# A planned order for the state-space mixer, and where the rows of the modulation are summed

## The chip, the cores and the metric

The kernel runs on one core of a Trainium2 chip. The metric is the time of one execution on the device, in microseconds (us). Three runs of the kernel before the change are shown, and one more execution was taken with the profiler. Engine names are those of the profile: PE is TensorE (PEld its weight loads), DVE is VectorE, ACT is ScalarE, POOL is GpSimd, SP is SyncE, which only issues transfers here.

## The reference

Two layers over a sequence of 1024 rows with 1024 channels, batch 1, all in float32. Each layer has a token mixer and a squared-ReLU MLP, both behind an RMS norm that is modulated by a vector c.

```
cs = silu(c)
for i in range(2):
    mod = cs @ w_ada[i] + b_ada[i]                      # 6 rows of 1024
    sh1, sc1, gt1, sh2, sc2, gt2 = split(mod, 6)
    h = rmsnorm(x, norm_mix[i]) * (1 + sc1) + sh1
    y = s5_mixer(h, ...) if i == 0 else gla_mixer(h, ...)
    x = x + gt1 * y
    h = rmsnorm(x, norm_mlp[i]) * (1 + sc2) + sh2
    x = x + gt2 * (relu(h @ w_ff1[i]) ** 2 @ w_ff2[i])
return rmsnorm(x, norm_final)
```

The mixer of layer 0 (S5) is a diagonal complex state-space layer: 64 groups of 16 channels, each with 64 complex states. It ends with a gated product: z = gelu(y), (val, gate) = split(z @ w_glu, 2), val * sigmoid(gate), where w_glu is 1024 x 2048.

## The kernel before, in words

The work runs through four large stages on one core: the mixer of layer 0 (up to some 170 us of the span), its gated product (to some 390 us), the two MLPs with the mixer of layer 1 between them. Matrix products of full precision are made of three products of split operands (a high and a low half, `split`, L106: ScalarE copies the high half, VectorE subtracts it for the low one).

**The mixer's steps.** The mixer is cut into eight blocks of eight groups each. The work on a block is written as generators whose steps run one at a time, and a string, `S5ORD` (L739), says in which order: each word is a letter and a block, and each time that it comes up the next step of that generator is traced. Inside the brackets the instructions of VectorE, ScalarE, GpSimd and TensorE stand in exactly this order in each engine's queue; an engine that meets a step whose input isn't there waits, with all that is queued behind it. The letters, with the engines of their steps in order:

- `g` (`group`, L511; b is a quarter, 0 to 3): 1 TensorE, 64 matmuls of c with four tiles of w_ada; 2 ScalarE copies; 3 TensorE transposes; 4 VectorE, three small operations; 5 TensorE, a small matmul; 6 ScalarE copies the scale and shift of the groups of two blocks, `gs`.
- `u` (`feed`, L544): 1 ScalarE, eight copies of x by rms into a `wk` buffer; 2 TensorE, eight transposes; 3 ScalarE, eight scalings by `gs` into U.
- `e` (`tab_e`, L573): 1 and 2 VectorE, two products each; 3 and 4 VectorE, a difference each, into E.
- `l` (`tab_lb`, L591): 1 and 2 VectorE, two products each into a `stg` buffer; 3 TensorE, 32 transposes and sums into two `tp` banks of PSUM; 4 ScalarE, two copies into LBT.
- `k` (`tab_k`, L619): 1 TensorE, 32 small products into two `tp` banks; 2 ScalarE, two copies into Ks; 3 VectorE, one small sum; 4 ScalarE issues the write of Ks to `kd` in memory; 5 ScalarE issues the read of `kd` as Tb.
- `p` (`rotation`, L486): 1 VectorE, a sum of phases; 2 VectorE, two operations that take off whole turns; 3 ScalarE, sine, absolute value and sine into the tile rot.
- `s` (`states`, L647): 1 ScalarE, R; 2 TensorE, 32 products of LBT and U; 3 VectorE, four products with rot; 4 VectorE, two sums; 5 VectorE, two scans; 6 VectorE, four products with rot into X.
- `o` (`output`, L691): 1 TensorE, 16 products with Tb; 2 TensorE, 64 products with X and E; 3 ScalarE, two Gelus into z.
- `S`, `T`, `H`, `I`: squares of x, the rms, the phases and the input matrices, once each.

The tag `tp` has two banks of PSUM and `mm` six. The tag `pz` has nine buffers: the last nine of the sixteen tiles of w_ada that the groups read (the last one of group 1, four of group 2, four of group 3) have them first, and then the tiles rot and z take them in turn as they come free. The tag `stg` has three buffers of 128 x 1056 (a load into one moves 512 KB).

**The gated product** (L905 to L939) runs over four quarters j of the columns and eight tiles t of 128 rows. A tile is 24 matmuls of 128 x 512 (`tok_mm`), a sigmoid on ScalarE and products on VectorE. The weights of a quarter come through `stg` (`glu_weights`, eight loads into four tiles in turn), and are split by ScalarE (wh) and VectorE (wl). Before j = 0, and during it, `ztrans` transposes z on TensorE, two groups of four for each tile, and splits it into hT.

**The rows of the modulation.** Two of the 6 rows of layer 0 are made by `group`. Ten rows remain for the list `ADA` (L904); the first six are made in the gated product: (0,2), (1,0), (0,3), (0,4), (0,5), (1,1), each a pair of layer and row. `ada_sum` (L173) loads eight tiles of 128 x 1024 of w_ada through `stg` and adds them up, weighted by silu(c), on VectorE into the tile adacc (one buffer, tag nrow). `ada_row` (L183) sums adacc over the partitions with four matmuls on TensorE (L191), adds the bias on VectorE into a `wk` buffer and, for (0,4) and (1,1), loads a row of norm weights into the same single buffer nrow and multiplies by it; then it writes the row to memory, mod. gt1 (row (0,2)) is read from there after j = 0, the scale and shift of the MLP (rows (0,4) and (0,3)) after j = 2.

Outside the brackets of S5ORD a planner orders the instructions when the kernel is built: at each point an engine takes, of the instructions that its own estimate holds to be ready, the one that was traced first. So the place of a call in the loop is a rank rather than a position. The queues are fixed after that.

Of the kernel before, what the change touches and what calls it, by code (L numbers as in the profile page):

```python
# [43 lines left out]
def trunk_kernel(ctx, tc, x, c, w_ada, b_ada, norm_mix, norm_mlp, s5_a_re, s5_a_im, s5_log_dt, s5_b_re, s5_b_im,  # L44
# [10 lines left out]
    def tt(out, a, b, op, e=None):  # L55
        (e or V).tensor_tensor(out=out, in0=a, in1=b, op=op)  # L56
# [8 lines left out]
    def act(out, a, f, **kw):  # L65
        S.activation(out=out, in_=a, func=f, **kw)  # L66
# [4 lines left out]
    def bank(tag="mm"):  # L71
        return ps.tile([P, 512], F32, tag=tag, name=tag, bufs={"mm": 6, "tp": 2}[tag])
# [40 lines left out]
    def row(src, tag="row", bufs=3, pool="ww"):  # L113
        t = pools[pool].tile([P, 1024], F32, tag=tag, name="row", bufs=bufs)
        nc.sync.dma_start(out=t, in_=src.to_broadcast([P, 1024]))
        return t
# [3 lines left out]
    def openp(name, side):  # L120
        pools[name] = tc.alloc_tile_pool(name=name, bufs=1, side=side, reuse_waits="tile")
        return pools[name]
# [50 lines left out]
    def ada_sum(l, j):  # L173
        acc = pools["ww"].tile([P, 1024], F32, tag="nrow", name="adacc", bufs=1)
        for kt in range(KT):
            w = stage(w_ada[l, kt * P:(kt + 1) * P, 1024 * j:1024 * (j + 1)])
            if kt == 0:
                ts(acc, w, csil[:, 0:1], ALU.mult)
            else:
                stt(acc, w, csil[:, kt:kt + 1], acc, ALU.mult, ALU.add)  # L180
        return acc

    def ada_row(l, j, acc):  # L183

        bt = wk()[:64, :512]
        for q in range(2):
            nc.sync.dma_start(out=bt[32 * q:32 * q + 32, :],
                              in_=b_ada[l:l + 1, 1024 * j + 512 * q:1024 * j + 512 * q + 512].to_broadcast([32, 512]))
        pst = bank()
        for q in range(2):  # L190
            T.matmul(pst[32 * q:32 * q + 32, :], ones, acc[:, 512 * q:512 * (q + 1)], start=True, stop=True)  # L191
        tt(bt, pst[:64, :], bt, ALU.add)
        if (l, j) in scales:
            n = pools["ww"].tile([P, 1024], F32, tag="nrow", name="nrow", bufs=1)[:64, :512]
            for q in range(2):
                nc.sync.dma_start(out=n[32 * q:32 * q + 32, :],
                                  in_=scales[l, j][:, 512 * q:512 * q + 512].to_broadcast([32, 512]))
            stt(bt, bt, 1.0, n, ALU.add, ALU.mult)
        for q in range(2):
            nc.sync.dma_start(out=modr[l][j][:, 512 * q:512 * q + 512], in_=bt[32 * q:32 * q + 1, :])  # L200
# [111 lines left out]
    def small(shape, dt=F32):  # L312
        n_s[0] += 1
        return sp.tile(shape, dt, name=f"s{n_s[0]}")
# [47 lines left out]
    s1 = small(sh1)  # L362
# [23 lines left out]
    s2 = small(sh1)  # L386
# [343 lines left out]
    def glu_weights(j, k2s=range(4)):  # L730
        wg = []
        for k2 in k2s:
            src = s5_w_glu[0, 2 * k2 * P:(2 * k2 + 2) * P, :].rearrange("(k p) (v n) -> p k v n", p=P, v=2)
            h, l = wsplit(None, [(lambda a, k=k: a.rearrange("p (k v n) -> p k v n", k=2, v=2)[:, k],
                                  src[:, k, :, 256 * j:256 * j + 256]) for k in range(2)])
            wg += [(h[:, 512 * k:512 * k + 512], l[:, 512 * k:512 * k + 512]) for k in range(2)]
        return wg

    S5ORD = "[ s0 s1 S7 S6 I0 S2 S3 e0 I0 S5 H1:v S0 S4 S1 e0 T0 H0:v T0 g0 l0 u0:am p0:v e0 e1 g0 g0 e0 u0 g0 u1:am e1 g0 l0 g1 g0 e1 u0 p0 k0 e1 e2 k0 p1:v g1 l0 p0 k0 e2 p1 e2 k0 p1 g2 l1 e2 l0 l1 g2 g1 e3 g2 s0 g1 g2 g1 g3 s0 g1 k0 g2 u1 g2 g3 e3 k1 u2:am e3 s0 k1 u1 l1 k1 s0 k1 p2:v s2 o0 s0 l1 g3 s1 g3 l2 g3 o0 s1 g3 k1 l2 k2 o0 e3 u2 p2 s1 k2 p2 l2 k2 s1 e4 k2 u2 o1 s1 l2 l3 o1 u3:am e4 l3 k2 s3 p3:v k3 e4 o1 s2 p3 e4 u3 e5 k3 p3 l3 s2 u3 k3 s2 l4 k3 l3 s2 u4:am k4 s3 e5 k4 s2 o2 s4 u4 l4 k3 o2 u5:am s3 u4 e5 l4 p4:v k4 e5 o2 p4 s3 k4 l4 e6 p4 k5 s3 s4 l5 o3 k5 s5 s3 u5 k4 u6:am e6 o3 l5 u5 s4 l5 o3 e6 p5:v k5 e6 k5 p5 l5 s4 p5 k6 e7 s5 s4 u6 k6 u7:am o4 l6 s4 k5 s6 u6 e7 o4 l6 s5 l6 o4 e7 p6:v k6 p6 k6 l6 e7 s5 p6 k7 s6 l7 s5 u7 k7 u7 o5 l7 s5 l7 k6 s7 s6 o5 l7 p7:v k7 p7 k7 s6 p7 s7 s6 o5 s7 o6 k7 s6 s7 o6 s7 s7 o6 o7 o7 o7 ]"  # L739

    kinds = {"u": feed, "l": tab_lb, "e": tab_e, "k": tab_k, "p": rotation, "s": states, "o": output, "g": group, "I": inputs}
    gen = {}
# [1 line left out]
    last = {}  # L744
    for n, w in enumerate(S5ORD.split()):
        if w[1:] != "7":
            continue
        last[w[0]] = n
    for n, w in enumerate(S5ORD.split()):
        if w == "[":  # L750
# [34 lines left out]
    def ztrans(t):  # L785
        for q in range(2):
            pt = bank("tp")
            for k in range(4):
                T.transpose(pt[:, P * k:P * k + P], zt[4 * q + k][:, t, :], ident)
            put(zT, t)(q, pt.rearrange("p (k t) -> p k t", k=4))  # L790
# [9 lines left out]
    def tok_mm(pst, hT_, t, w, cs=slice(None)):  # L800
        hh, hl = (hT_[i][:, t] for i in range(2))
        for kt in range(KT):
            mm3(pst, hh[:, kt, :], hl[:, kt, :], w[kt][0][:, cs], w[kt][1][:, cs], kt == 0, kt == KT - 1)
# [61 lines left out]
    def first_half(side):  # L865

        br = openp("br", side)
        return [[br.tile([P, 4, 512], F32R, name=f"{n}{q + 1}1") for n in "hl"] for q in range(2)]

    def second_half(side):  # L870
        return openp("rw", side).tile([P, 2, 4, 512], F32, name="raw")

    def put_block(R, t, xv, g, sh, e=V):

        tk = slice(P * (t % 4), P * (t % 4) + P)

        def evac(q, src):
            if t < 4:
                split(R[q][0][:, :, tk], R[q][1][:, :, tk], src)
            elif q:  # L880
                act(R[2][:, 1, :, tk], src, AF.Copy)
            else:
                tt(R[2][:, 0, :, tk], src, R[2][:, 1, :, tk], ALU.subtract)
        return norm_T(stg()[:, :1024], xv, g, sh, evac, (0, 1) if t < 4 else (1, 0), e)
# [13 lines left out]
    def gated(t, js, u):  # L898

        tt(u, u, gt1[:, js], ALU.mult)  # L900
        xv = xb[:, 7 - t, js]
        tt(xv, xv, u, ALU.add)

    ADA = [(0, 2), (1, 0), (0, 3), (0, 4), (0, 5), (1, 1), (1, 2), (1, 3), (1, 4), (1, 5)]  # L904
    for j in range(4):  # L905
        if j > 0:
            wg = glu_weights(j)
        js = slice(256 * j, 256 * j + 256)
        for t in range(NT):
            pst = bank()  # L910
            tok_mm(pst, zT, t, wg)
            if j == 0:
                if t + 2 < NT:
                    ztrans(t + 2)
                sg = held[t // 4][:, 256 * (t % 4):256 * (t % 4) + 256]
            else:
                sg = pools["ww"].tile([P, 256], F32, tag="sg", name="sg", bufs=3)
            if j < 3 and t in (1, 5):
                acc = ada_sum(*ADA[0])
            if j < 3 and t in ((4, 7) if j == 2 else (3, 7)):  # L920
                ada_row(*ADA.pop(0), acc)
            act(sg, pst[:, 256:], AF.Sigmoid)
            tt(sg, pst[:, 0:256], sg, ALU.mult)
            if j > 0:
                gated(t, js, sg)
            if j == 3:
                xv = xb[:, 7 - t, :]
                put_block(R, t, xv, g2, sh2)
        if j == 0:
            zp.release()  # L930
            openp("mp", "right")
            gt1 = row(modr[0][2])
            for t in range(NT):
                gated(t, js, held[t // 4][:, 256 * (t % 4):256 * (t % 4) + 256])
        if j == 2:
            g2 = row(modr[0][4])
            sh2 = row(modr[0][3])
            pools["mp"].release()
            R = first_half("right") + [second_half("right")]  # L939
# [450 lines left out]
    for w in ORD.split():  # L1390
        t, j = int(w[1]), int(w[2:] or 0)
# [60 lines left out]
    g2 = row(modr[1][4])  # L1452
# [83 lines left out]
```

## Time and profile before

| what | value |
|---|---|
| median of 3 runs | 2189.99 us (2188.33 to 2190.81) |
| the profiled execution | 2189.98 us |
| its span, first to last instruction | 2188.3 us |
| PE busy | 2112.1 us (97%) |
| DVE busy | 1447.4 us (66%) |
| ACT busy | 692.9 us (32%) |
| POOL busy | 397.0 us (18%) |
| mean granted clock of TensorE | 0.987 |

The busy shares are means over stages with different bounds. The profile names lines of the kernel; many operations go through helpers (L56 a product, sum or difference of two tiles on VectorE, L59 a product with a scalar and a second operation, L63 one with a scalar, L66 an operation of ScalarE, L215 to L217 the three matmuls of a full product), so the tiles' names tell them apart. A row of the instructions in order of time gives start, length, engine, line, operation, output<-input, and in square brackets the idle time of the engine before it and what ended it. A row of the chain of waits gives start, length, engine or DMA, and tile and line.

### The profile page before, as it was taken

How to read it: one execution, taken by the hardware profiler on the slowest of the kernel's cores; microseconds unless marked ns; L12 is line 12 of the kernel's file. 1: busy time of each engine (PE TensorE's matmuls, PEld its weight loads, DVE VectorE, ACT ScalarE, POOL GpSimd, SP SyncE). 2: the span in 40 equal slices, each digit the busy share in tenths (PEclk: the TensorE clock that was granted, in tenths of full speed). 3: DMA queues.
4: the chain of work that ended last, by engine and by line, in shares of the span. 5: the costliest groups of instructions: out<-in, count | busy, mean ns of one | idle time of the engine just before them, and what ended most of it. 6: DMA issues, size and time to landing. Idle time of an engine off the chain costs nothing.

```text
span 2188.3 us, 26758 instructions
## 1 busy us (share of the span) xinstructions
PE 2112.1 (97%) x10857; PEld 1726.8 (79%) x10857; DVE 1447.4 (66%) x2004; ACT 692.9 (32%) x1163; POOL 397.0 (18%) x294
## 2 busy tenths in 40 slices
PE   5988999999999999999899999999999999999998
PEld 4887777788888888888687877787788888888886
DVE  8996767966656656656732366738875665665666
ACT  5772114322222222222511443314322222222223
POOL 0000001222213213222500000001122222222223
PEclk9999999999999999999899999999999999999999
DMA  8234670111111111112343114421111111111112
GB/s 257 57 89 166 228 241 23 39 58 58 49 49 58 49 49 58 49 49 75 132 144 100 49 34 143 150 77 38 41 48 49 58 48 49 58 49 49 58 49 106
DMA packets 107655, 176.58 MB, mean 81 GB/s; under 512 B 10462, under 2 KB 76102, under 8 KB 107468
## 3 DMA queue, kind: packets, MB, share of 16 engines
q1 hardware_dynamic: 97164, 168.71, 24.3%
q10 hardware_dynamic: 10368, 6.16, 1.3%
q8 instruction: 85, 1.39, 0.3%
q14 instruction: 38, 0.31, 0.0%
HBM read 164.45 MB, written 10.40 MB: 80 GB/s over the span
## 4 chain that ended last, share of the span: by engine, by line
PE 88%; DVE 6%; DMA 3%; ACT 2%; issue 1%; POOL 0%; SPq 0%; ACTq 0%; POOLq 0%; DVEq 0%
PE mm L216 27%; PE mm L215 27%; PE mm L217 27%; DMA stg<-in_w_ada_dram 1%; DVE tmp L56 1%; PE tp L609 1%; PE mm L1362 1%; PE tp L210 1%; PE mm L1342 1%; PE mm L704 1%; DMA stg<-in_s_w_glu_dram 0%; PE mm L658 0%; DVE adacc L59 0%; DMA stg<-in_gla_w_out_dram 0%; DVE nk L59 0%
## 5 line engine op out<-in xcount | busy, mean ns | idle before, releaser
L56 DVE TENSOR_TENSOR big<-mm,big 128x512 f32<-128x512 f32 x528 | 343.0, 684 | 91.3 <-PE mm L217 86.3
L216 PE MATMUL mm<-w,a 128*128 128x512 f32 x1024 | 386.7, 392 | 0.5 <-DVE w L56 0.5
L217 PE MATMUL mm<-w,a 128*128 128x512 f32 x1024 | 384.8, 390 | 0.0
L215 PE MATMUL mm<-w,a 128*128 128x512 f32 x1024 | 365.1, 390 | 2.6 <-ACT w L66 2.6
L216 PE MATMUL mm<-l,rg 128*128 128x512 f32 x904 | 356.3, 394 | 4.7 <-DVE l L56 4.7
L217 PE MATMUL mm<-h,rg 128*128 128x512 f32 x904 | 355.0, 393 | 0.5 <-DVE rg L56 0.5
L215 PE MATMUL mm<-h,rg 128*128 128x512 f32 x904 | 351.1, 394 | 2.4 <-ACT h L66 1.8
L56 DVE TENSOR_TENSOR wk<-mm,wk 128x512 f32<-128x512 f32 (+1 forms) x100 | 68.8, 688 | 381.5 <-PE mm L217 312.5
L215 PE MATMUL mm<-wh,hT 128*128 128x512 f32 (+1 forms) x768 | 291.1, 381 | 2.5 <-ACT hT L66 1.7
L56 POOL TENSOR_TENSOR wk<-wk 128x512 f32<-128x512 f32 (+1 forms) x122 | 160.3, 1324 | 732.3 <-DVE wl L56 307.4
L217 PE MATMUL mm<-wh,hT 128*128 128x512 f32 (+1 forms) x768 | 290.3, 378 | 0.0
L216 PE MATMUL mm<-wl,hT 128*128 128x512 f32 (+1 forms) x768 | 289.6, 378 | 0.1
L56 POOL TENSOR_TENSOR wk<-wk,row 128x1024 f32<-128x1024 f32 x64 | 163.1, 2549 | 610.2 <-DMA wk<-in_w_ff_dram 405.4
L216 PEld LDWEIGHTS mm<-w,a 128*128 128x128 f32 x1024 | 192.3, 188 | 46.4 <-DVE w L56 7.3
L215 PEld LDWEIGHTS mm<-w,a 128*128 128x128 f32 x1024 | 191.3, 188 | 44.6 <-ACT w L66 3.5
L217 PEld LDWEIGHTS mm<-w,a 128*128 128x128 f32 x1024 | 192.3, 188 | 39.1
L66 ACT ACTIVATE wk<-mm 128x512 f32<-128x512 f32 x140 | 83.4, 597 | 422.7 <-PE mm L217 419.0
L216 PEld LDWEIGHTS mm<-l,rg 128*128 128x128 f32 x904 | 170.6, 189 | 43.1 <-DVE l L56 5.6
L215 PEld LDWEIGHTS mm<-h,rg 128*128 128x128 f32 x904 | 170.2, 188 | 41.5 <-ACT h L66 2.3
L217 PEld LDWEIGHTS mm<-h,rg 128*128 128x128 f32 x904 | 170.5, 189 | 39.0 <-DVE rg L56 0.8
L66 ACT ACTIVATE rg<-wk 128x1024 fp32r<-128x1024 f32 (+1 forms) x126 | 114.2, 952 | 266.1 <-POOL wk L56 264.7
L215 PEld LDWEIGHTS mm<-wh,hT 128*128 128x128 f32 x768 | 144.7, 189 | 40.1 <-issue 3.9
(244 smaller groups left out, 2615.8 us busy)
## 6 DMA issues: line engine op xcount, KB each, us to landing
wk<-in_w_ff_dram SPq DMA_DIRECT2D x128, 512.0 KB
stg<-in_w_ada_dram SPq DMA_DIRECT2D x80, 512.0 KB
stg<-in_gla_w_in_dram SPq DMA_DIRECT2D x17, 512.0 KB
stg<-in_s_w_glu_dram SPq DMA_DIRECT2D x32, 256.0 KB
row<-mod SPq DMA_DIRECT2D x10, 512.0 KB
wada<-in_w_ada_dram SPq DMA_DIRECT2D x9, 512.0 KB
big<-in_x_dram SPq DMA_DIRECT2D x8, 512.0 KB
Tb<-kd ACTq DMA_DIRECT2D x8, 512.0 KB
```

Source lines behind the costliest of these rows:

```text
L56: (e or V).tensor_tensor(out=out, in0=a, in1=b, op=op)
L66: S.activation(out=out, in_=a, func=f, **kw)
L210: ins = T.transpose(pt[:, P * k:P * k + P], h[:, P * (4 * q + k):P * (4 * q + k + 1)], ident)
L215: T.matmul(pst, ah, bh, start=first, stop=False, **kw)
L216: T.matmul(pst, ah, bl, start=False, stop=False, **kw)
L217: return T.matmul(pst, al, bh, start=False, stop=last, **kw)
L609: T.matmul(pts[i][:, P * q:P * q + P], t[i][k][:, P * q:P * q + P], (nident if i < k else ident), start=q == 0 and k == 0, stop=q == 3 and ...
L704: T.matmul(Yp[r][:, P * q:P * q + P], X[rr, i, q, :], E[rr, i // 2, q, :], start=False, stop=(q == 3 and i == 3))
L1342: T.matmul(kvp[c2][hp2][:, 256 * (h % 2):256 * (h % 2) + 256], kz[t % 2][cr, P * h:P * h + P], vo[cr, t, 256 * h:256 * h + 256], start=Tru ...
L1362: T.matmul(op[h // 2][64 * c2:64 * c2 + 64, 256 * (h % 2):256 * (h % 2) + 256], qT[:, h, n0:n0 + 64], Sc[c2][:, h, :], start=True, stop=True)
```

## The change

Two things. The string S5ORD is replaced by another order of the same words (262 of them between the brackets' ends, each as often as before). And the calls of `ada_sum` and `ada_row` stand at other tiles of the gated product: the sums were at tiles 1 and 5 of j = 0, 1 and 2, the rows at tiles 3 and 7 (4 and 7 in j = 2). Now j = 0 has one sum (tile 4) and one row (7), j = 1 two sums (0, 4) and two rows (2, 7), and j = 2 three sums (0, 2, 5) and three rows (1, 4, 7). The order of the rows in ADA stays.

```diff
@@ -736,7 +736,7 @@
             wg += [(h[:, 512 * k:512 * k + 512], l[:, 512 * k:512 * k + 512]) for k in range(2)]
         return wg
 
-    S5ORD = "[ s0 s1 S7 S6 I0 S2 S3 e0 I0 S5 H1:v S0 S4 S1 e0 T0 H0:v T0 g0 l0 u0:am p0:v e0 e1 g0 g0 e0 u0 g0 u1:am e1 g0 l0 g1 g0 e1 u0 p0 k0 e1 e2 k0 p1:v g1 l0 p0 k0 e2 p1 e2 k0 p1 g2 l1 e2 l0 l1 g2 g1 e3 g2 s0 g1 g2 g1 g3 s0 g1 k0 g2 u1 g2 g3 e3 k1 u2:am e3 s0 k1 u1 l1 k1 s0 k1 p2:v s2 o0 s0 l1 g3 s1 g3 l2 g3 o0 s1 g3 k1 l2 k2 o0 e3 u2 p2 s1 k2 p2 l2 k2 s1 e4 k2 u2 o1 s1 l2 l3 o1 u3:am e4 l3 k2 s3 p3:v k3 e4 o1 s2 p3 e4 u3 e5 k3 p3 l3 s2 u3 k3 s2 l4 k3 l3 s2 u4:am k4 s3 e5 k4 s2 o2 s4 u4 l4 k3 o2 u5:am s3 u4 e5 l4 p4:v k4 e5 o2 p4 s3 k4 l4 e6 p4 k5 s3 s4 l5 o3 k5 s5 s3 u5 k4 u6:am e6 o3 l5 u5 s4 l5 o3 e6 p5:v k5 e6 k5 p5 l5 s4 p5 k6 e7 s5 s4 u6 k6 u7:am o4 l6 s4 k5 s6 u6 e7 o4 l6 s5 l6 o4 e7 p6:v k6 p6 k6 l6 e7 s5 p6 k7 s6 l7 s5 u7 k7 u7 o5 l7 s5 l7 k6 s7 s6 o5 l7 p7:v k7 p7 k7 s6 p7 s7 s6 o5 s7 o6 k7 s6 s7 o6 s7 s7 o6 o7 o7 o7 ]"
+    S5ORD = "[ s0 s1 S7 S6 I0 S2 S3 e0 I0 S5 H1:v S0 S4 S1 e0 T0 H0:v T0 g0 l0 u0:am p0:v e0 p0 g0 g0 e0 u0 p0 g0 l0 g0 e1 g1 g0 u1:am p1:v e1 k0 p1 k0 g1 l0 u0 k0 e1 e2 e1 e2 k0 p1 g2 l1 l0 e2 l1 g2 g1 g2 s0 g1 g2 e2 g1 g2 s0 u1 g1 k0 g2 k1 u2:am g3 p2:v s0 k1 g3 l1 u1 k1 s0 p2 k1 s2 o0 l1 s0 p2 g3 s1 g3 l2 g3 o0 g3 s1 k1 l2 k2 o0 s1 u2 e3 k2 u2 s1 l2 k2 e3 k2 u3:am o1 p3:v e3 p3 l2 e3 p3 s1 k3 s2 l3 k2 k3 o1 s3 s2 l3 u3 o1 k3 s2 l3 e4 k3 u3 s2 l3 e4 o2 u4:am p4:v e4 s3 p4 k3 e4 p4 u4 s2 k4 l4 k4 o2 s4 s3 u4 l4 o2 k4 s3 l4 e5 k4 u5:am s3 l4 e5 o3 s5 p5:v e5 s4 p5 k4 e5 u5 p5 s3 k5 l5 k5 o3 u5 s4 u6:am l5 k5 s4 l5 o3 e6 s4 k5 l5 e6 o4 s6 p6:v e6 s5 p6 e6 u6 p6 s4 k6 l6 k5 o4 k6 u6 s5 u7:am l6 k6 s5 l6 o4 e7 s5 k6 l6 e7 o5 s7 p7:v e7 s6 p7 e7 u7 p7 s5 k7 l7 k6 o5 k7 u7 s6 l7 o5 k7 s6 l7 k7 s6 o6 l7 s6 s7 o6 s7 k7 s7 o6 s7 s7 o7 o7 o7 ]"
 
     kinds = {"u": feed, "l": tab_lb, "e": tab_e, "k": tab_k, "p": rotation, "s": states, "o": output, "g": group, "I": inputs}
     gen = {}
@@ -915,9 +915,9 @@
                 sg = held[t // 4][:, 256 * (t % 4):256 * (t % 4) + 256]
             else:
                 sg = pools["ww"].tile([P, 256], F32, tag="sg", name="sg", bufs=3)
-            if j < 3 and t in (1, 5):
+            if (j, t) in ((0, 4), (1, 0), (1, 4), (2, 0), (2, 2), (2, 5)):
                 acc = ada_sum(*ADA[0])
-            if j < 3 and t in ((4, 7) if j == 2 else (3, 7)):
+            if (j, t) in ((0, 7), (1, 2), (1, 7), (2, 1), (2, 4), (2, 7)):
                 ada_row(*ADA.pop(0), acc)
             act(sg, pst[:, 256:], AF.Sigmoid)
             tt(sg, pst[:, 0:256], sg, ALU.mult)
```

## The prediction

> **What bounds the kernel now.** I read the page first, then stretches of 20 us, then the chain of waits, and last each engine's instructions in order of time around the two places that the diff touches.
>
> ```profile
> span 2188.3 us, 26758 instructions
> ...
> PE 2112.1 (97%) x10857; PEld 1726.8 (79%) x10857; DVE 1447.4 (66%) x2004; ACT 692.9 (32%) x1163; POOL 397.0 (18%) x294
> ```
>
> TensorE is busy for 97% of the span, so time can only come from, or go into, the few places where it waits. Here is the part that the diff touches (columns: stretch, length, busy time of each engine, granted clock, DMA share, GB/s):
>
> ```profile
> 20.00:40.00 20.00, 11.45 (x171) 8.78 (x171) 19.55 (x41) 14.13 (x39) 1.97 (x1) 1.00 1.09 349
> ...
> 120.00:140.00 20.00, 18.71 (x269) 17.04 (x269) 19.93 (x32) 17.36 (x38) 0.00 (x0) 1.00 0.32 80
> 140.00:160.00 20.00, 14.30 (x169) 13.43 (x169) 15.72 (x26) 10.86 (x18) 0.00 (x0) 0.88 0.56 124
> ...
> 200.00:220.00 20.00, 20.00 (x97) 15.66 (x96) 12.63 (x17) 4.35 (x9) 0.00 (x0) 1.00 0.44 154
> ```
>
> Up to some 150 us (the mixer's steps) VectorE is the bound: 19.93 of 20 us. From 180 us on (the gated product) it is TensorE: 20.00 of 20, with VectorE at two thirds. So in the mixer a wait of VectorE costs its length; in the gated product only a wait of TensorE does.
>
> **The change, part by part. First the mixer's order.** Both orders hold the same 262 words, so VectorE's work is the same, and only its waits differ. The old order's large waits:
>
> ```profile
> 51.40 2.48 DVE L56 TENSOR_TENSOR tmp<-mm,rot 128x512 f32<-128x512 f32 x4 [1.35 <-PE mm L658]
> ...
> 155.23 2.48 DVE L56 TENSOR_TENSOR tmp<-mm,rot 128x512 f32<-128x512 f32 x4 [4.25 <-ACT rot L66]
> ```
>
> The second goes: p7 now stands before k7, so rotation 7 is ready some 13 us of VectorE work before s7 uses it: -4.25. In its place s7 meets another. After l7's second step VectorE has k7 (0.1), s6's sums (1.2), scans (2.25) and four products (2.4), 6.0 us in all; TensorE has l7 (3.78, row below), o6's 16 products (1.8) and s7's 32 (1.9), 7.5 us: a new wait of +1.5. The last read of kd also comes about 0.5 us too late for o7, an estimate from its write of 6.31 us: +0.5.
>
> ```profile
> 130.35 3.78 PE tp L609 x32
> ...
> 147.12 6.31 DMA kd<-Ks
> ```
>
> The first wait gets worse, and this is the point of the order that I trust most. The chain of waits over the start:
>
> ```profile
> 33.09 1.21 DVE tmp L56 x2
> ...
> 36.09 3.43 PE mm L518 x64
> 39.52 0.61 PE tp L628 x31
> ...
> 40.15 0.29 ACT Ks L66
> ...
> 40.48 3.84 PE tp L609 x32
> 44.32 1.02 PE mm L518 x30
> ...
> 45.37 1.16 ACT rot L66 x2
> ...
> 46.55 0.72 ACT rot L66
> 47.27 0.97 ACT LBT L66 x2
> ...
> 48.79 2.93 PE mm L658 x32
> ```
>
> ```profile
> 31.64 2.43 ACT L66 ACTIVATE wk<-big,s 128x128 f32<-128x128 f32 x8
> ...
> 45.37 1.15 ACT L66 ACTIVATE rot<-tmp 128x512 f32<-128x512 f32 x2 [2.81 <-PE mm L518]
> ```
>
> Rotation 1 waited 2.81 us, until half of group 2's matmuls (1.02 us) was through. The code says why: the rotations and the nine last weights of the groups share the nine buffers pz. Rotation 0 gets the buffer of group 1's last weight, rotation 1 that of group 2's first. In the old order p0's third step stands behind group 1's matmuls; in the new one it stands ahead of them. ScalarE runs its queue in order, so it sits at rotation 0 until 39.52. Behind it are queued rotation 0 (1.88), the copy of group 0 (0.2), u1's eight copies (2.43, in the old order long done) and the first copy of Ks (0.29): Ks is there at 44.32 instead of 40.44. VectorE, which has products of 0.60 each and comes to k0's third step at about 40.5 (8.7 us of steps from 31.8), waits 3.9 us there, and l0's transposes start 3.88 us later, since they need the two PSUM banks that Ks leaves. From there the old chain runs on: 51.72 + 3.88 = 55.6 for the end of s0's products. TensorE has by then sat idle for 4 us, and such a wait slows what follows:
>
> ```profile
> 90.64 1.56 PE L628 MATMUL tp<-E,BB 64*32 64x128 f32 x32 [2.82 <-ACT LBT L66]
> ```
>
> (1.56 us for what took 0.61 above.) I allow -1.0 to +3.2 for the clock, since the old 2.93 of s0 was at the lower clock already, and take 56.5 (54.6 to 58.8). That is 5.1 after the old 51.40, and VectorE has done 1.2 us less by then (g3's and e3's steps come later): the early shift is +6.3 (4.4 to 8.6). Sum of the order: 6.3 - 4.25 + 1.5 + 0.5 = **+4** (2 to 6). If rotation 0 did not wait: -1.35 - 4.25 + 2.0 = -3.6.
>
> **Second, the sums.** The old places of the six rows' matmuls, and of the two sums in the third quarter of the gated product (j = 2):
>
> ```profile
> 229.52 1.05 PE L191 MATMUL mm<-adacc,ones 128*32 128x512 f32 x4
> ...
> 255.20 1.05 PE L191 MATMUL mm<-adacc,ones 128*32 128x512 f32 x4
> ...
> 278.56 1.05 PE L191 MATMUL mm<-adacc,ones 128*32 128x512 f32 x4
> ...
> 307.43 1.05 PE L191 MATMUL mm<-adacc,ones 128*32 128x512 f32 x4
> ...
> 326.88 1.19 PE L215 MATMUL mm<-wh,hT 128*128 128x512 f32 x4 [0.62 <-ACT wh L66]
> ```
>
> ```profile
> 286.73 0.68 DVE L59 SCALAR_TENSOR_TENSOR wk<-wk,nrow 64x512 f32<-64x512 f32 x1 [3.42 <-DMA nrow<-in_norm_mlp_dram]
> 287.45 0.75 DVE L63 TENSOR_SCALAR adacc<-stg,csil 128x1024 f32<-128x1024 f32 x1
> ...
> 302.96 1.28 DVE L59 SCALAR_TENSOR_TENSOR adacc<-stg,csil,adacc 128x1024 f32<-128x1024 f32 x1
> ...
> 309.47 0.73 DVE L63 TENSOR_SCALAR adacc<-stg,csil 128x1024 f32<-128x1024 f32 x1
> ...
> 322.80 1.28 DVE L59 SCALAR_TENSOR_TENSOR adacc<-stg,csil,adacc 128x1024 f32<-128x1024 f32 x1 [0.76 <-DMA stg<-in_w_ada_dram]
> ```
>
> Read as: a row's matmuls run at their place in the code, since TensorE always has work ahead of them. The accumulator adacc has one buffer, so a sum starts only after the row before it (307.43 + 1.05, next sum at 309.47). A sum takes 302.96 + 1.28 - 287.45 = 16.8 us or 322.80 + 1.28 - 309.47 = 14.6; VectorE needs only eight steps of 1.28, the rest is waiting for stg, three buffers of 512 KB. I take S = 15.7. And the weights of the last quarter share stg behind the last sum: it ends at 324.08, and j = 3 starts 2.8 us later with a wait for these weights. That chain is the second bound of this stage, with little slack already.
>
> The diff puts one row into j = 0, two into j = 1, three into j = 2. The fourth row, which needs the nrow buffer too, goes from (1,7) to (2,1), and so two sums and that row stand where one sum stood, between (1,7) and (2,4). New chain: the third row's matmuls at (1,7) end at 279.61, less one row that is no longer ahead (1.05), less 1.5 gained at the start of j = 1 (its first four tiles took 255.20 - 230.57 = 24.6 us, the last four 278.56 - 256.25 = 22.3; the weights come earlier when one sum fewer stands before them): 277.06. Then 1.0 to the fourth sum, S, the fourth row (1.05, and 279.61 to 287.45 = 7.84 to the next sum), S, the fifth row (2.04), S, and 2.8 to the weights (a row's write to mod waits on SP's queue ahead of the next sum's loads; that is in the measured gaps): 291.8 + 3S = 338.9. The old j = 3 starts at 326.88: **+12.0** (8.7 at 14.6, 15.3 at 16.8). TensorE has no other work to put there: the eight tiles end near 325.
>
> At nothing I cost: gt1, which now comes after (0,7), not (0,3); the first tiles of j = 1 fill six PSUM banks before TensorE waits, and without that cover it would cost a row's way, some 8 us. And the first sum's move from tile 1 to tile 4:
>
> ```profile
> 174.24 0.75 DVE L63 TENSOR_SCALAR adacc<-stg,csil 128x1024 f32<-128x1024 f32 x1 [4.90 <-DMA stg<-in_w_ada_dram]
> ...
> 178.59 1.09 PE L789 MATMUL tp<-ident,z 128*128 128x128 f32 x4 [4.12 <-DVE hT L56]
> ```
>
> The sum waits for its load in VectorE's queue with the first tile's hT behind it, and TensorE waits 4.12 for that. But the planner already pulled it ahead of everything up to tile 1, and a place at tile 4 does not forbid that; if it did, up to -4.1.
>
> The profiled execution took 2189.98 us, which is the median of the runs shown (2189.99). Sum: 2189.98 + 4 + 12 = **2206 us**.
>
> **Rivals.** (1) The sums fit. The DMA moved 349 GB/s in 20 to 40 us; eight times 512 KB at that rate are 12.0 us, the chain ends at 327.8, and the loss there is 0.9: 2195. Against it: three buffers never gave a sum under 14 us. The Trainium skill, "DMA: Bandwidth & Descriptors", Specifications, puts the limit of one core's HBM traffic at about 358 GB/s; an estimate by that figure is 11.7 us for a sum and 2194 us for the kernel. The 349 GB/s of the first row agrees with it, but there the loads don't wait for three buffers. (2) Rotation 0 does not wait and the chain stands: 2189.98 - 3.6 + 12 = 2198. Against it: the 2.81. (3) Faster: the new order pays in full. Place: VectorE at 51 and 155 us, -5.6, with s7's wait hidden under an earlier l7. It decides from the point where 291.8 + 3S - 326.88 is below 1.2, that is S under 12.1: 2185 at most. For it: VectorE's waits are the mixer's only loss. (4) The change does nothing in the gated product, because the planner keeps the sums where they were: then only the order counts, 2194. Against it: rows stood at their places in the code each time.
>
> **How the numbers follow.** The forecast 0.58, its own range 2200 to 2213; rival 1 0.10; rival 2 0.15; rival 3 0.10; rival 4 0.07. Range for 8 in 10: 2190 to 2214, which leaves out rival 3 and a chain in which TensorE also stands at a row's matmuls. 0.2% is 4.4 us, about what a measurement of this kernel can tell from no change. Below 2185.6: rival 3 and a tail, 0.12. Within 4.4: rival 4 and half of rival 1, 0.13. Above: 0.75.
>
> **What would show it.** Right: ScalarE's first rot waits some 4 us for L518, VectorE's first product on rot starts at 56 to 57 instead of 51.4, no 4 us wait for rot near the end; six rows' matmuls with the fourth and fifth some 26 us apart or more; j = 3's first products over 10 us late, after a wait for wh. Wrong: sums of 12 us or fewer, or a first rot that starts near 36.

## The result, and the profile after

The changed kernel took 2212.11 us (median of 4 runs, 2209.53 to 2212.9) against 2189.26 (4 runs) of the kernel before beside it: a ratio of 1.0102, interval 1.0084 to 1.0119. It is slower by 22.9 us. Its profiled execution took 2209.53 us, the shortest of the four, so the trace can explain 19.5 us (span 2207.8 against 2188.3) and not the other 3. The head of the page after:

```profile
span 2207.8 us, 26759 instructions
...
PE 2119.2 (96%) x10857; PEld 1729.1 (78%) x10857; DVE 1451.2 (66%) x2004; ACT 692.7 (31%) x1163; POOL 396.4 (18%) x294
```

Stretches of 20 us of the changed kernel (columns as before, the granted clock in the third place from the end):

```profile
40.00:60.00 20.00, 14.68 (x241) 12.94 (x234) 12.73 (x27) 12.46 (x38) 0.00 (x0) 0.83 0.33 101
...
240.00:260.00 20.00, 15.60 (x61) 11.53 (x60) 16.92 (x32) 0.77 (x2) 0.00 (x0) 0.91 0.62 200
...
300.00:320.00 20.00, 19.37 (x74) 14.46 (x75) 10.87 (x16) 0.77 (x2) 0.00 (x0) 0.87 0.73 257
320.00:340.00 20.00, 16.25 (x64) 12.13 (x64) 14.82 (x17) 1.15 (x3) 0.00 (x0) 0.91 0.74 251
```

The first stretch is the early wait of the mixer. The other three are in the gated product, where TensorE had been busy for 20.00, 20.00 and 19.31 of 20 us at clock 1.00: it now misses 4.40 us in the first of them, 0.63 in the second and 3.75 in the third, and its mean clock is 0.87 to 0.91 in all three.

The mixer's order, in ScalarE's instructions of the changed kernel in order of time:

```profile
39.74 1.15 ACT L66 ACTIVATE rot<-tmp 128x512 f32<-128x512 f32 x2 [7.47 <-PE mm L518]
...
43.97 0.41 ACT L66 ACTIVATE Ks<-tp 128x128 f32<-128x128 f32 x2
...
51.58 1.15 ACT L66 ACTIVATE rot<-tmp 128x512 f32<-128x512 f32 x2 [4.25 <-PE mm L518]
```

and in VectorE's:

```profile
44.48 0.19 DVE L56 TENSOR_TENSOR Ks<-Ks,skip 128x32 f32<-128x32 f32 x1 [3.43 <-ACT Ks L66]
...
54.38 0.16 DVE L56 TENSOR_TENSOR s<-tp,s 128x4 f32<-128x4 f32 x1 [3.09 <-PE tp L527]
...
56.73 2.48 DVE L56 TENSOR_TENSOR tmp<-mm,rot 128x512 f32<-128x512 f32 x4 [0.50 <-PE mm L658]
...
159.10 2.48 DVE L56 TENSOR_TENSOR tmp<-mm,rot 128x512 f32<-128x512 f32 x4 [0.84 <-PE mm L658]
```

Rotation 0 waits for group 1's matmuls, Ks is late behind it, VectorE waits 3.43 us for Ks and later 3.09 for TensorE, which is late by the same chain, and the first product on rot starts at 56.73 (51.40 before). The wait of 4.25 us near the end is gone; 0.84 stands in its place.

The gated product, in TensorE's instructions: the restart after the mixer, the six rows, and the first product of j = 3.

```profile
179.44 1.11 PE L789 MATMUL tp<-ident,z 128*128 128x128 f32 x4 [2.59 <-DVE hT L56]
...
231.16 1.05 PE L191 MATMUL mm<-adacc,ones 128*32 128x512 f32 x4
253.44 1.23 PE L191 MATMUL mm<-adacc,ones 128*32 128x512 f32 x4 [4.40 <-DVE adacc L59]
283.88 1.05 PE L191 MATMUL mm<-adacc,ones 128*32 128x512 f32 x4
300.63 1.92 PE L191 MATMUL mm<-adacc,ones 128*32 128x512 f32 x4 [4.41 <-DVE adacc L59]
324.41 1.05 PE L191 MATMUL mm<-adacc,ones 128*32 128x512 f32 x4 [3.75 <-DVE adacc L59]
343.76 1.05 PE L191 MATMUL mm<-adacc,ones 128*32 128x512 f32 x4
344.74 1.19 PE L215 MATMUL mm<-wh,hT 128*128 128x512 f32 x4
```

Before, no row's matmuls waited. Now three of six do: 4.40, 4.41 and 3.75 us, with the next tiles queued behind them. The restart is 0.85 later than before (178.59), j = 3 starts 17.86 later (326.88), and what follows takes 2207.8 - 344.74 = 1863.1 us instead of 1861.4. These two sums make up the span: 17.86 + 1.7 = 19.5.

VectorE's sums in the changed kernel, first the second sum, then the three of j = 2:

```profile
232.87 0.74 DVE L63 TENSOR_SCALAR adacc<-stg,csil 128x1024 f32<-128x1024 f32 x1
...
241.05 2.77 DVE L56 TENSOR_TENSOR held<-held,row 128x256 f32<-128x256 f32 x8 [1.87 <-DMA row<-mod]
...
252.02 1.27 DVE L59 SCALAR_TENSOR_TENSOR adacc<-stg,csil,adacc 128x1024 f32<-128x1024 f32 x1
...
285.92 0.74 DVE L63 TENSOR_SCALAR adacc<-stg,csil 128x1024 f32<-128x1024 f32 x1
...
299.20 1.28 DVE L59 SCALAR_TENSOR_TENSOR adacc<-stg,csil,adacc 128x1024 f32<-128x1024 f32 x1 [0.81 <-DMA stg<-in_w_ada_dram]
305.76 0.69 DVE L59 SCALAR_TENSOR_TENSOR wk<-wk,nrow 64x512 f32<-64x512 f32 x1 [2.49 <-DMA nrow<-in_norm_mlp_dram]
306.48 0.75 DVE L63 TENSOR_SCALAR adacc<-stg,csil 128x1024 f32<-128x1024 f32 x1
...
322.99 1.27 DVE L59 SCALAR_TENSOR_TENSOR adacc<-stg,csil,adacc 128x1024 f32<-128x1024 f32 x1
326.11 0.73 DVE L63 TENSOR_SCALAR adacc<-stg,csil 128x1024 f32<-128x1024 f32 x1
...
340.47 1.28 DVE L59 SCALAR_TENSOR_TENSOR adacc<-stg,csil,adacc 128x1024 f32<-128x1024 f32 x1 [0.60 <-DMA stg<-in_w_ada_dram]
```

Start of the first row to end of the last: the second sum takes 252.02 + 1.27 - 232.87 = 20.4 us, the three in j = 2 take 14.6, 17.8 and 15.6. Inside the second sum stand the products of gt1 on the first quarter (`held` by `row`), and a wait of 1.87 us for gt1 itself.

### The profile page after: what moved, and what is told of

Same layout as the page of the kernel before. It is cut to its first block, busy times and chain, and to the rows that moved or that the text cites. A ratio compares the mean times of both kernels' runs of the same rounds, so it can differ in the third digit from the quotient of the medians.

```text
span 2207.8 us, 26759 instructions
## 1 busy us (share of the span) xinstructions
PE 2119.2 (96%) x10857; PEld 1729.1 (78%) x10857; DVE 1451.2 (66%) x2004; ACT 692.7 (31%) x1163; POOL 396.4 (18%) x294
## 4 chain that ended last, share of the span: by engine, by line
PE 81%; DVE 6%; DMA 3%; POOL 1%; ACT 1%; issue 1%; POOLq 0%; SPq 0%; DVEq 0%
PE mm L215 26%; PE mm L216 26%; PE mm L217 26%; DMA stg<-in_w_ada_dram 2%; PE mm L1362 1%; PE tp L210 1%; DVE adacc L59 1%; DVE big L56 1%; PE mm L1342 1%; DVE nk L59 1%; DVE l L56 1%; DMA wk<-in_w_ff_dram 1%; POOL wk L56 1%; PE mm L191 0%; DMA stg<-in_gla_w_out_dram 0%
```

## The experiments

In one table (the before beside each group of runs lies between 2189.12 and 2190.48 us; the restart, TensorE's first long run after the mixer, and the sixth row's matmuls are given by their starts in the one profiled execution):

| kernel | median us | ratio to before, interval | restart | sixth row |
|---|---|---|---|---|
| before | 2189.26 | | 178.59 | 325.21 |
| changed | 2212.11 | 1.0102 (1.0084 to 1.0119) | 179.44 | 343.76 |
| e1 order only | 2193.74 | 1.0018 (1.0008 to 1.0027) | 181.16 | 328.72 |
| e2 sums only | 2210.92 | 1.0094 (1.0079 to 1.0109) | 179.44 | 343.34 |
| e3 order, rotation 0 late | 2188.02 | 0.9992 (0.9982 to 1.0002) | 176.87 | 323.23 |
| e4 changed, half sums in j = 2 | 2196.19 | 1.0024 (1.0013 to 1.0036) | 180.22 | 334.74 |
| e5 before, first sum held | 2186.22 | 0.9982 (0.9973 to 0.9991) | 175.22 | 322.46 |
| e6 changed, second row later | 2205.79 | 1.0070 (1.0056 to 1.0084) | 180.97 | 341.95 |
| e7 e3 and k7 earlier | 2189.37 | 0.9999 (0.9990 to 1.0007) | 178.12 | 325.69 |
| e8 e7 and first sum held | 2184.78 | 0.9973 (0.9965 to 0.9982) | 173.35 | 320.05 |
| e9 changed, gt1's products traced later | 2211.91 | 1.0101 (1.0084 to 1.0117) | 180.37 | 345.64 |
| e10 changed, gt1's products tied later | 2205.31 | 1.0069 (1.0053 to 1.0086) | 181.75 | 342.68 |

**e1 and e2: each half of the change alone.** e1 is the kernel before with the new S5ORD; e2 is the changed kernel with the old one.

> The new order alone, the sums at their old places. Theory (the sums' chain costs most of it): the mixer's early wait is there (VectorE's first product on rot at 56 to 57 us) and the late one is gone; TensorE's first long run of the gated product starts about 1 us later than before (179.4 against 178.6), and the kernel takes 2190 to 2192 us, 0 to 2 above before. Rival (the order is what costs): 2205 or more, most of the 20 us.

> The old order, the sums and rows at their new places. Theory: the last quarter's first products (wh, j = 3) start some 17 us later than before, at 343 to 345 us, and the kernel takes 2206 to 2211 us. Rival (the order is what costs): within 4 us of before.

The medians move by +3.3 us (e1) and +20.5 (e2), together 23.8 against 22.9 for both: the halves add up, and the sums are six sevenths of it. e2 came as expected (j = 3 at 344.32). e1 came out above what was expected of it: its restart is 2.6 later than before, not 0.8. TensorE's instructions of e1:

```profile
166.87 3.63 PE L696 MATMUL mm<-Tb,U 128*128 128x128 f32 x16 [2.74 <-DMA Tb<-kd]
...
181.16 1.11 PE L789 MATMUL tp<-ident,z 128*128 128x128 f32 x4 [3.19 <-DVE hT L56]
```

The read of kd is late for o7 by 2.74 us, where 0.5 had been forecast. The restart has to be read with care: e4, e6, e9 and e10 below differ from the changed kernel only in work behind it, and their restarts are still 0.8 to 2.3 us later than its own (their waits for the read of kd are 2.78 to 5.30 us, against 2.71).

**e3: the early wait taken away.** p0's third step behind group 1's matmuls, all else as in e1:

```diff
- e0 u0 p0 g0 l0 g0 e1 g1 g0 u1:am p1:v e1 k0 p1 k0 g1 l0 u0 k0
+ e0 u0 g0 l0 g0 e1 g1 g0 u1:am p1:v e1 k0 p1 k0 g1 l0 u0 p0 k0
```

> As the first kernel (new order, old places of the sums), but p0's third step, which writes rotation 0, stands behind group 1's matmuls and after u0's third step. Theory (ScalarE's queue stands at rotation 0 because its buffer in pz is still group 1's weight): the first rot has no wait of 7 us for L518, Ks is copied near 40 us, VectorE's wait of 3.4 us there goes, its first product on rot starts at 51 to 53 us, and the last products of the mixer end 3 to 5 us earlier than in the first kernel; the kernel takes 2186 to 2189 us. Rival (the wait has another cause, so the step's place is without effect): the same times as the first kernel within 1 us.

ScalarE's instructions of e3, then VectorE's:

```profile
40.52 0.45 ACT L66 ACTIVATE Ks<-tp 128x128 f32<-128x128 f32 x2 [1.97 <-PE tp L628]
43.75 1.21 ACT L66 ACTIVATE rot<-tmp 128x512 f32<-128x512 f32 x2
```

```profile
41.06 0.19 DVE L56 TENSOR_TENSOR Ks<-Ks,skip 128x32 f32<-128x32 f32 x1 [0.50 <-ACT Ks L66]
```

Rotation 0 finds its buffer free, Ks comes at 40.52 instead of 43.97, VectorE's wait falls from 3.43 (changed) to 0.50. The first product on rot starts at 53.24 (just outside the 51 to 53 expected). The time falls by 5.7 us from e1, to where it was before, within the interval. One word in 262 carries the whole loss of the order.

**e4: half of the three sums in j = 2.** They load and add four of their eight tiles, so those rows are computed only in part.

```diff
-    def ada_sum(l, j):
+    def ada_sum(l, j, n=KT):
-        for kt in range(KT):
+        for kt in range(n):
-                acc = ada_sum(*ADA[0])
+                acc = ada_sum(*ADA[0], n=4 if j == 2 else KT)
```

> The changed kernel, but each of the three sums in the third quarter (j = 2) adds up four of its eight tiles of w_ada only (the other four are neither loaded nor added). Theory (three sums in a row, each 15 to 18 us, with one accumulator, carry the third quarter): with sums of about 8 us TensorE's tiles end last, no wait of 4 us before the fourth and fifth row's matmuls, j = 3 starts near 331 to 333 us instead of 344.7, and the kernel takes 2197 to 2201 us. Rival (the wait comes from the weights' own loads, or from the rows' path through nrow and mod): j = 3 starts at 340 or later, 2207 or more.

TensorE's rows in j = 2 of e4:

```profile
299.20 1.05 PE L191 MATMUL mm<-adacc,ones 128*32 128x512 f32 x4
...
316.97 1.05 PE L191 MATMUL mm<-adacc,ones 128*32 128x512 f32 x4
...
334.74 1.05 PE L191 MATMUL mm<-adacc,ones 128*32 128x512 f32 x4
```

No row waits there, all at 1.05 us, and the time falls by 15.9 us, a little more than expected. From the end of the third row's matmuls (287.98) to j = 3 (335.73) it is 47.7 us instead of 59.8; j = 3 itself comes later than the 331 to 333 expected, since the third row does. So the length of these three sums is what that quarter pays for. About 6 us against the before beside it stay, of which the second row's wait is a part (4.02 us in e4 too).

**e5: the work in front of the restart.** The kernel before; the first sum is tied behind the first tile's hT: inside `issue_after` the planner places instructions only behind the one named (lo0, the last subtraction of that hT).

```diff
-                acc = ada_sum(*ADA[0])
+                with tc.issue_after(lo0) if len(ADA) == 10 else nullcontext():
+                    acc = ada_sum(*ADA[0])
```

> The kernel before (old order, old places), but the first sum's operations on VectorE are held behind the low halves of the first tile's hT. Theory (the first sum's wait for its load, with hT queued behind it, is what TensorE waits 4 us for): TensorE's long run starts near 175 us instead of 178.6, every later row's matmuls come 3 to 5 us earlier, and the kernel takes 2184 to 2187 us. Rival (hT is late for another reason, or the later sums then carry the end): within 1 us of before.

TensorE's restart in e5:

```profile
175.22 1.12 PE L789 MATMUL tp<-ident,z 128*128 128x128 f32 x4 [0.16 <-DVE hT L56]
```

The wait falls from 4.12 to 0.16 us and the time by 3.9; the later rows come some 2.7 us earlier, a little less than expected. So in the kernel before the first sum, not the mixer's end, set the restart, which is 3.4 us earlier with that sum held.

**e6: the second row one tile later.** The changed kernel with (1, 3) for (1, 2) in the list of rows.

> The changed kernel with one number changed: the second row stands at (1, 3) instead of (1, 2). Theory (the second sum takes some 20 us, since gt1's products on the first quarter now fall on it, and TensorE stands at the row's matmuls): the wait of 4.4 us there goes, the third row's matmuls run 4 to 6 us earlier (278 to 280 us), the chain of the third quarter with them, and the kernel takes 2205 to 2209 us. Rival (loads alone carry the third quarter, so an earlier start is without effect): 2211 to 2213 us.

TensorE's rows in e6:

```profile
256.05 1.05 PE L191 MATMUL mm<-adacc,ones 128*32 128x512 f32 x4
...
298.96 1.92 PE L191 MATMUL mm<-adacc,ones 128*32 128x512 f32 x4 [7.21 <-DVE adacc L59]
...
322.59 1.05 PE L191 MATMUL mm<-adacc,ones 128*32 128x512 f32 x4 [3.67 <-DVE adacc L59]
...
343.06 1.20 PE L215 MATMUL mm<-wh,hT 128*128 128x512 f32 x4
```

The wait of 4.40 is gone and the time falls by 6.3 us. But of the gain only 1.7 is left at j = 3: the third row is 4.5 earlier (279.41), and the fourth row's wait grows from 4.41 to 7.21. VectorE's instructions of e6 show where the rest goes:

```profile
281.12 1.22 DVE L56 TENSOR_TENSOR wl<-stg,wh 128x1024 fp32r<-128x1024 f32 x1
...
283.51 0.74 DVE L63 TENSOR_SCALAR adacc<-stg,csil 128x1024 f32<-128x1024 f32 x1
```

The fourth sum starts at 283.51, 3.1 us after the third row's matmuls end (280.46), where it was 1.0 in the changed kernel: VectorE is still at the end of j = 1, with the last split of the weights of j = 2 among its work. The sum then takes 15.3 us instead of 14.6, and the fourth row is only 1.7 earlier than in the changed kernel. Some 3 us more come after j = 3 (2203.2 - 343.06 = 1860.1 against 1863.1); why isn't known, but over the kernels here that part varied from 1859.4 us (e4) to 1863.5 (e9).

**e7 and e8: a version that beats both.** e7 is e3 with k7's steps 2 to 4 earlier, so that the read of kd comes earlier; e8 is e7 with e5's tie.

```diff
- s5 k7 l7 k6 o5 k7 u7 s6 l7 o5 k7 s6 l7 k7 s6 o6
+ s5 k7 k7 l7 k6 k7 o5 k7 u7 s6 l7 o5 s6 l7 s6 o6
```

> As the kernel with rotation 0 behind group 1 (new order, old places of the sums), but k7's second, third and fourth steps some 5 us earlier in ScalarE's queue (ahead of u7's eight copies). Theory (o7's first products wait 3 us for the read of kd, which waits for its write): that wait goes, z7 ends 3 us earlier; but the first sum's load still ends last, so TensorE's run starts at most 1.5 us earlier and the kernel takes 2186 to 2188 us. Rival (z7 carries the start of the run): 3 us less, 2184 to 2185.

> The last kernel with the first sum held behind the first tile's hT: new order, rotation 0 behind group 1, k7 early, the sums at their old places. Theory: with neither the load of the first sum nor o7's wait in front, TensorE's run starts near 172 to 173 us, 6 us before the 178.6 of the kernel before, and the kernel takes 2182 to 2185 us. Rival (the sums of the later quarters then carry j = 3): 2186 to 2189.

TensorE in e7:

```profile
162.12 2.05 PE L696 MATMUL mm<-Tb,U 128*128 128x128 f32 x16 [1.30 <-DMA Tb<-kd]
...
178.12 1.12 PE L789 MATMUL tp<-ident,z 128*128 128x128 f32 x4 [4.84 <-DVE hT L56]
```

and in e8:

```profile
173.35 1.11 PE L789 MATMUL tp<-ident,z 128*128 128x128 f32 x4 [0.15 <-DVE hT L56]
```

In e7 o7 still waits 1.30 us for the read, of 3.00 in e3. The last transposes of z ahead of the restart start at 169.11, 2.5 us sooner than in e3 (171.63), and yet the restart is 1.2 later: TensorE waits 4.84 us there for hT, behind the first sum, and neither the expected gain of e7 nor its rival's came. With the sum held (e8) the restart is 5.24 us before that of the kernel before, and the time 5.4 below (2190.16 beside it): faster than both kernels. Of the 5.4 the tie alone gave 3.9 (e5).

**e9 and e10: what made the second sum 20.4 us long.** Both move gt1's sixteen products on the first quarter to (1, 3), behind the second row; e10 also ties them to the last step of the second sum.

```diff
+            if (j, t) == (1, 3):
+                with tc.issue_after(lasts[0].ins):        # e10 only
+                    for i in range(NT):
+                        gated(i, slice(0, 256), held[i // 4][:, 256 * (i % 4):256 * (i % 4) + 256])
...
-            for t in range(NT):
-                gated(t, js, held[t // 4][:, 256 * (t % 4):256 * (t % 4) + 256])
```

> The changed kernel with one move: the sixteen products and sums of gt1 on the first quarter, which followed j = 0, are traced behind tile 3 of j = 1, that is behind the second row. In the changed kernel they stand among the second sum's steps (2.77 + 1.08 + 1.75 us of VectorE, and 1.87 us of wait for gt1 ahead of them), that sum takes 20.4 us and TensorE stands 4.40 us at the second row's matmuls. Theory (VectorE sets that sum): it shrinks by 4 to 6 us to about 15 us, the wait at the second row falls below 1.5 us, and the time is 2206 to 2210. Rival (the loads of the sum set it, the products only fill VectorE's gaps): the sum stays above 18 us, the wait above 3 us, and the time is 2211 to 2213.

> As the move of gt1's products tried before, which left them where they stood since a call's place is only a rank; now the sixteen products and sums of gt1 on the first quarter are tied behind the last step of the second sum, so that on VectorE they really follow it. Theory (VectorE sets the second sum of the changed kernel, 20.4 us): it shrinks to 14 to 16 us, TensorE's wait of 4.40 us at the second row's matmuls falls below 1 us, and the time is 2206 to 2210. Rival (the loads through the three stg buffers set it): the sum stays above 18 us and the wait above 3 us, and the time is 2211 to 2213.

e9 tells nothing of the sum: the planner put the products where they had been, among its steps, and the time did not move. In e10 they follow it. VectorE's second sum in e10, then TensorE's rows:

```profile
235.08 0.73 DVE L63 TENSOR_SCALAR adacc<-stg,csil 128x1024 f32<-128x1024 f32 x1
...
249.88 1.28 DVE L59 SCALAR_TENSOR_TENSOR adacc<-stg,csil,adacc 128x1024 f32<-128x1024 f32 x1 [0.37 <-DMA stg<-in_w_ada_dram]
```

```profile
251.31 1.05 PE L191 MATMUL mm<-adacc,ones 128*32 128x512 f32 x4
...
280.20 1.05 PE L191 MATMUL mm<-adacc,ones 128*32 128x512 f32 x4
...
298.64 1.92 PE L191 MATMUL mm<-adacc,ones 128*32 128x512 f32 x4 [6.10 <-DVE adacc L59]
```

The sum takes 249.88 + 1.28 - 235.08 = 16.1 us, the row's matmuls wait for nothing, and the time falls by 6.8 us, a little below the range expected. So gt1's products, and the wait for gt1 ahead of them, made the second sum long. As in e6 a large part of the gain is gone by the fourth row, which waits 6.10: the fourth sum starts at 284.19, 2.9 us after the third row's matmuls end.

## Why the prediction was right and wrong

Right was that it is slower, and both places. The forecast of 2206 us is 3.5 below the profiled execution and 6 below the median; 2212.11 lies within the range of 2190 to 2214, near its upper end. That the total came so near is in part luck: at the start of j = 3 the sums cost 5.0 us more than the 12 forecast, and at the restart 0.85 stands where the order's 4 was forecast.

- **The early wait: right, and shown** by e3. Forecast were a first rot at 39.5, 3.9 us of wait at Ks and a first product on rot at 56.5; measured 39.74, 3.43 and 56.73. Of the signs one was off here: rotation 0 waited 7.47 us, not some 4, since ScalarE was through with its earlier work at 32.27. The wait of 4.25 went, as said; s7 waits 0.84, where 1.5 was forecast.
- **The order's +4: the right size at the mixer's end, but not what the restart pays.** e1 alone gave +3.3 us (by its interval 1.8 to 5.9), and its last transposes of z ahead of the restart start 4.2 later (175.44 against 171.24). But the read of kd was mis-sized (0.5 forecast, 2.74 measured in e1), and the mixer's end was taken to set the restart. e5 shows that in the kernel before the first sum did; in e1 the restart is 2.6 late, not 4.2. In the changed kernel it is 0.85 late, and even that can't be put down to the order: e2, with the old order, restarts at the same 179.44.
- **The sums' +12: 5.0 too small at j = 3, and the step that failed is "at nothing I cost" gt1 after (0,7).** The cover named, six PSUM banks, looked only at TensorE's wait for gt1. But gt1's products also fell among the second sum's steps on VectorE, which made it 20.4 us long instead of 15.7; TensorE, which runs in order, reached that sum's row, at (1,2), 8.0 us after gt1 had come (249.04 against 241.05), and stood 4.40 at it. Its next five tiles were slower as well (29.2 us from that row to the third, 27.8 in e10). So the chain did not start at 277.06 but at 284.93, the end of the third row; less the 0.85 of the restart that is 7.0 late. e10 and e6 show that 6.0 of it is this step: with the products tied behind the sum, or the row one tile later, the third row comes 98.4 us after the restart instead of 104.4. The other 1.0 lies ahead of the second row and is not explained. Of the 6.0 only 3.3 reach j = 3 (165.3 us after the restart in the changed kernel, 162.1 and 161.9 in e6 and e10, 148.3 before), since with the third row in time the fourth sum waits for VectorE: the forecast's 1.0 us to that sum would have been some 3. The prediction's own last lines left out "a chain in which TensorE also stands at a row's matmuls"; three rows did that.
- **The chain of three sums in j = 2: right up to the fifth row, and shown** by e4, where the same stretch is 12.1 us shorter with half the sums. Forecast were 61.8 us from the third row to j = 3; measured 344.74 - 284.93 = 59.8. S was 16.0 in the mean (15.7 taken). The fourth row's way to the next sum was 306.48 - 302.55 = 3.9 us, not 7.84. The last link agrees by luck: it was to be the sixth sum and 2.8 us to the weights (18.5 in all), but that sum ends at 341.75, 2.0 us ahead of its row, and j = 3 doesn't wait for wh; it follows straight on the sixth row's matmuls. TensorE's own three tiles, some of them at the lower clock, take those 18.3 us. TensorE loses the time at the fourth and fifth rows (4.41 and 3.75) and to the lower clock behind them. Two signs were wrong: the wait for wh, and the fourth and fifth rows 26 us apart or more (23.8).
- **In one sum**, at the start of j = 3: forecast 4 + 12 = +16, measured +17.86 = 0.85 (restart) + 7.0 (late chain) + 12.0 - 2.0 (chain). The other 1.7 us of the span fell behind j = 3 and are not explained, nor are the 3 us between the profiled execution and the median.
- **Rival 1 (sums at the full rate of the DMA)** fell: no sum of j = 2 took under 14.5 us, in either kernel; 251 and 257 GB/s were moved in the changed kernel's two stretches there. The Trainium skill, "DMA: Bandwidth & Descriptors", Specifications, gives about 358 GB/s as the limit; the measurement stands for three buffers in turn. Rival 2 fell to rotation 0's wait of 7.47, rival 4 to the rows' new places (283.88, 300.63, 324.41), and rival 3 needed S under 12.1 as well as no early wait.

## What to carry to other kernels

Where work is moved to "later" places, count for each stage what passes through its serial resources (here one accumulator, three load buffers) and also what else runs on the engine that feeds them just there; a wait on an engine that runs in order is paid by all that is queued behind it. An order that a planner makes needs to know of buffers that different kinds of tile share: one word ahead of the release of its buffer cost 5.7 us. Before pricing a delay at the end of a stage, ask what else the next stage's start waits for: here the first sum's load hid 1.6 of the 4.2 us by which e1's mixer was late, and made a mixer that was 2.5 us earlier worth nothing until that sum was held. And before pricing a wait that goes, ask what comes next: of 6.0 us gained at the third row 3.3 were left at j = 3.

## What the runs showed of the hardware

The clock of TensorE falls at moments that the length of the wait before doesn't tell. In e2 a wait of 2.54 us was followed at once by slow matmuls (TensorE's instructions of e2: four in 1.92 us instead of 1.05, and 0.80 for what takes 0.39):

```profile
324.12 1.92 PE L191 MATMUL mm<-adacc,ones 128*32 128x512 f32 x4 [2.54 <-DVE adacc L59]
325.97 0.80 PE L215 MATMUL mm<-wh,hT 128*128 128x512 f32 x1
...
327.35 0.39 PE L215 MATMUL mm<-wh,hT 128*128 128x512 f32 x1
```

In the changed kernel the longer wait of 3.75 us at 324.41 was followed by four matmuls at full speed, and the slow ones came 1 to 2 us later:

```profile
325.39 0.51 PE L215 MATMUL mm<-wh,hT 128*128 128x512 f32 x1
...
326.48 0.63 PE L215 MATMUL mm<-wh,hT 128*128 128x512 f32 x1
```

And in e9 a wait of 3.61 us, at the same fifth row, was followed by no slow matmuls at all (327.84 1.05, then 0.50 and from there on 0.39 and 0.40).

The Trainium skill, "TensorE: Matmul & The Clock Gate", Part 1, has the clock set by how busy the engine was in a free-running window of about 3.4 us. That waits of 2.54, 3.61 and 3.75 us were followed by slow matmuls at once, not at all and with a delay fits such a window, but no run here shows the window itself. The advice in the section "Why this matters for your kernels" of that page of the Trainium skill, no idle gaps above some 3 us, is no safe bound here: 2.54 us already cost.
